# Second block's gate products: whole sums and weights' low parts by adding transfers; the last attention head at a denser pace

## The chip, the cores and the metric

One core of one Trainium2 chip runs the kernel. The metric is the device time of one execution in microseconds (us), the median of three runs. The engines are named as in the profile: PE is TensorE, DVE is VectorE, ACT is ScalarE, POOL is GpSimd, SP is SyncE, which only issues transfers here.

## The reference

Two transformer blocks follow one another, on 1024 positions of width 1024, all in float32. The change touches only the mixing part of the second:

```python
def second_block(x, ...):
    h = rms_norm_2(x, norm_mix_g)
    proj = h @ w_in
    (c_val, c_gate, g_q, g_k, g_v, g_og, g_f, d_q, d_k, d_v,
     m_conv, m_gla, m_diff) = jnp.split(proj, IN_OFFSETS, axis=-1)
    o_conv = conv_module(c_val, c_gate, ...)      # depthwise conv of 31, layer norm, silu, product
    o_gla = gla(g_q, g_k, g_v, g_og, g_f, ...)    # gated linear attention, 4 heads
    o_diff = diff_attention(d_q, d_k, d_v, ...)   # two softmaxes a head, 8 heads, rms norm of the output
    y = sigmoid(m_conv) * o_conv + sigmoid(m_gla) * o_gla + sigmoid(m_diff) * o_diff
    x = x + y @ w_out
    ...                                           # feed-forward, final norm
```

## The kernel before

Activations lie transposed in SBUF: a tile has 128 features on the partitions and 1024 positions along them, or a half of 512. A float32 operand is split into a high part, rounded to the matmul's type (`F32R`), and a low part, the rest. `mm3` makes a product of two split operands with three matmuls (high by high, high by low, low by high), so one 128x128 block of weights on 512 positions costs three matmuls. Two helpers make the parts. `split` (L379 to L382) casts on ScalarE and subtracts on VectorE or GpSimd. `split_dma` (L384 to L389) casts on ScalarE, lets ScalarE write the negated high part into the low part's tile, and lets GpSimd issue a transfer that adds the source to it.

The second block's mixing part has three stages. `diff` makes the differential attention and the projections that it and the convolution need. Its TensorE order is written by slots: a slot is half a product (12 matmuls), and `plan` hangs the steps of a head on slots: `scores`, three slots later `trans`, five later `pv` for every second block of queries, then `norm_sums` (it squares the head's output into `osq` and sums its columns on TensorE) and `norm_rows` (VectorE copies the factors to `bc`, TensorE turns them to rows `prow`). The other engines are ordered there by a planner, which works with its own costs. The last head has 24 slots; its norm rows hung on slots behind them.

`Gates` is next. It makes the remaining projections as 18 pairs of weight blocks, each pair by seven products of half size in place of eight. Products are taken of sums and differences of the blocks of the weights (`s1` to `s4`) and of the activations (`t1` to `t4`). `weights` makes one pair's: `part` splits two halves into a pair of tiles `hi`, `lo` (four buffers), `s2`, `s3`, `s4` are GpSimd's sums of raw weights, `w1` to `w4` call `part`. Raw weights have three buffers, filled in order by SP. `up` begins the stage: the activations lie split in `h`, so `full` adds the two parts of a block to a whole one (`g`, `a` in the profile), the differences are made on VectorE and split again. In between TensorE makes the forget gate's product (`forget`) and its four groups (`forget_up`, evacuated by ScalarE at L2481). `loop` then runs over the pairs, with the parts for the next pair made beside the products. In `Gates` the five engines' queues, SP's too, keep the order in which the program issues.

`Gla`, the gated linear attention, follows. The pools of `Gates` lie where those of `diff` were, so a tile of the one is free when the last reader of the other is done: `g1` and `g5` lie over the tile of `osq`.

The lines on which the change bears most, of `up` as it was:

```python
        W[0]["w1"]()
        f = self.forget_weights()
        sums(0)
        for t in ("s2", "s3", "s4"):
            W[0][t]()
        self.forget(*f)
        W[1]["w1"]()
        W[2]["w1"]()
        self.forget_up(0)
        sums(1)
        ...
        W[0]["w2"]()
        self.prod(0, 0)
```

Of the kernel before, what the change touches and what calls it, by code (L numbers as in the profile page):

```python
# [11 lines left out]
F32 = mybir.dt.float32  # L12
# [4 lines left out]
ALU = mybir.AluOpType  # L17
# [49 lines left out]
class Split:  # L67


    def __init__(self, pool, n, tag, halves=(0, 1)):  # L70
        self.pool, self.tag = pool, tag
        self.t = {h: [None] * n for h in halves}
        for h in halves:
            for i in range(n):
                self.make(h, i)
# [5 lines left out]
    def half(self, k, h):  # L81
        return self.t[h][k]
# [7 lines left out]
class Rope:  # L90
# [23 lines left out]
    def load(self, g, px, py):  # L114

        sx, sy, x, y = [self.tmp() for _ in range(4)]
        self.raw(px, self.net.v("qn_gx", 0), x, sx)
        for i, p in enumerate(py if isinstance(py, list) else ()):
            hs = slice(i * H, i * H + H)
            self.raw(p, self.net.v("qn_gy", 0), y[:, hs], sy[:, hs])  # L120
        if not isinstance(py, list):
            self.raw(py, self.net.v("qn_gy", 0), y, sy)
        self.xy[g] = x, sx, y, sy
# [161 lines left out]
class Net:  # L285
# [708 lines left out]
    def diff(self, hl, st, pre):  # L994
# [198 lines left out]
        def plan(h, base, pace):  # L1193

            s = [base + 4 + round(pace * qb) for qb in range(8)]
            for c in range(2):
                at(base + 3 + 2 * c, values, h, c)
            for qb in range(8):
                at(s[qb], scores, h, qb)
                at(s[qb] + 3, trans, h, qb)  # L1200
                if qb % 2:
                    at(s[qb] + 5, pv, h, qb // 2)
            at(s[7] + 7, norm_sums, h)
            at(s[7] + 12, norm_rows, h, 0)
            at(s[7] + 13, norm_rows, h, 1)

        def run(blocks):

# [24 lines left out]
        with tc.manual_schedule(engines={nc.tensor.engine}):  # L1233
            self.slot = -1
            run([("dq", 0), ("dk", 0)])
            self.slot = 0
            base = 0
            for h in range(8):
                blocks = head_blocks(h)
                plan(h, base, (1.5 if h == 0 else 1.7) if h in (0, 7) else 2)  # L1240
                run(blocks)
                base += 4 * len(blocks)
            for x in sorted(events):
                for f in events[x]:
                    f()
# [20 lines left out]
class Ending:  # L1266
# [17 lines left out]
    def plan(self, m, at, xT, tmp):  # L1284


        self.xT, self.tmp = xT, tmp
        at(0, lambda: self.net.w_fetch(3))
        for ct, x in enumerate((3 * m, 3 * m, 4 * m, 4 * m + 1)):
            at(x, lambda ct=ct: self.stat(0, ct))  # L1290
        at(5 * m - 1, self.warm)
        at(5 * m, lambda: self.stats(0, 4, 5))
        at(5 * m + 1, lambda: self.stats(0, 6, 7))
# [241 lines left out]
class Ffn:  # L1535
# [4 lines left out]
    UP = [("a11", "b11", "x", True), ("s2", "t2", "y", True), ("a12", "b21", "x", False), ("s3", "t3", "y", False),  # L1540
          ("s1", "t1", "z", True), ("a22", "t4", "y", False), ("s4", "b22", "z", False)]

    def __init__(self, net, g, nf, first_block, side):
        self.net, self.nc, self.g, self.nf, self.first_block = net, net.nc, g, nf, first_block
        self.side, self.other = (side, "left" if side == "right" else "right")
        self.xd = [net.dram.tile([P, S], F32, name=f"xd{nf}_{i}") for i in range(CT)]
        self.gd = [net.dram.tile([P, S], F32, name=f"gd{nf}_{i}") for i in range(nf)]
        self.n = 0
# [74 lines left out]
    def weights(self, j, A):  # L1623

        net, e = self.net, self.nc.gpsimd
        lo, hi = slice(0, H), slice(H, S)
        r, s = [], []

        def raw(i):
            while len(r) <= i:  # L1630
                net.w_fetch(1)
                r.append(net.wq_raw.pop(0)[1])
            return r[i]

        def part(names, srcs):
            h = net.whl.tile([P, S], F32R, tag="hi", name="whi")
            l = net.whl.tile([P, S], F32R, tag="lo", name="wlo")
            for o, src in srcs:
                net.split(h[:, o], l[:, o], src, e)
            for n, o in zip(names, (lo, hi)):  # L1640
                A[n] = h[:, o], l[:, o]

        def s2():
            s.extend(self.fw.tile([P, S], F32, tag=t, name=t) for t in ("sa", "sb"))
            self.tt(e, s[1][:, lo], raw(1)[:, lo], raw(1)[:, hi])
            self.tt(e, s[0][:, lo], s[1][:, lo], raw(0)[:, lo], ALU.subtract)
            net.w_fetch(1)

        def s3():
            self.tt(e, s[0][:, hi], r[0][:, lo], r[1][:, lo], ALU.subtract)  # L1650

        def s4():
            self.tt(e, s[1][:, hi], r[0][:, hi], s[0][:, lo], ALU.subtract)

        return {"w1": lambda: part(("a11", "a12"), [(lo, raw(0)[:, lo]), (hi, raw(0)[:, hi])]), "s2": s2, "s3": s3, "s4": s4,
                "w2": lambda: part(("s2", "s3"), [(slice(0, S), s[0])]),
                "w3": lambda: part(("s1",), [(lo, s[1][:, lo])]),
                "w4": lambda: (part(("s4", "a22"), [(lo, s[1][:, hi]), (hi, r[1][:, hi])]), net.w_fetch(2))}

# [744 lines left out]
class Gates(Ffn):  # L2404

    def __init__(self, net, hl, st):
        self.net, self.nc, self.hl, self.st = net, net.nc, hl, st
        self.nf = len(PAIRS)  # L2410
        self.more = []
        self.seen = set()
        self.n = 0
        self.other = "right"
        tiles = lambda n, m, w=S: [net.dram.tile([P, w], F32, name=f"{n}{i}") for i in range(m)]
        net.decd = tiles("decd", 4, 16)
        self.zd, net.xqd, net.xkd, net.kdd = [tiles(n, 4) for n in ("zd", "xqd", "xkd", "kdd")]
        net.gvd = [tiles(f"gvd{g}", 2) for g in range(4)]
        net.god = tiles("god", CT)
# [64 lines left out]
    def up(self):  # L2484
        net, nc, B, hl = self.net, self.nc, self.B, self.hl
        v, p = nc.vector, nc.gpsimd
        for k in range(4):
            for n, i, half in (("b11", k, 0), ("b21", k + 4, 0), ("b22", k + 4, 1), ("t1", k, 1)):
                B.setdefault(n, []).append(hl.half(i, half))
        self.pairs = {}  # L2490
        W = {}

        def new(j):
            A = {}
            W[j] = self.weights(j, A)
            self.pairs[j] = {"A": A}

        def full(e, o, x):
            self.tt(e, o, x[0].bitcast(F32), x[1].bitcast(F32))

        sub = lambda o, x, y: self.tt(v, o, x, y, ALU.subtract)
        half = lambda t: (t[:, 0:H], t[:, H:S])
        temps = half(self.big(1))
        t1 = half(self.big(5)) + half(self.T("a5"))

        def sums(k):
            x21, x22 = half(self.big(k % 2 * 4))
            x12 = temps[k % 2]
            full(p, x22, B["b22"][k])
            full(p, x21, B["b21"][k])  # L2510
            full(v if k < 2 else p, x12, B["t1"][k])
            full(v if k < 2 else p, t1[k], B["b11"][k])
            sub(t1[k], x12, t1[k])
            sub(x12, x22, x12)
            sub(x22, x22, t1[k])
            sub(x21, x21, x22)
            for n, t in (("t3", x12), ("t2", x22), ("t4", x21)):
                net.split(*B[n][k], t)

        for j in range(EARLY):  # L2520
            new(j)
        W[0]["w1"]()
        f = self.forget_weights()
        sums(0)
        for t in ("s2", "s3", "s4"):
            W[0][t]()
# [5 lines that stand above are left out]
        self.forget_up(1)  # L2532
        sums(2)
        self.forget_up(2)
        sums(3)
        W[0]["w2"]()
        self.prod(0, 0)

        for k in range(4):
            net.split(*B["t1"][k], t1[k])  # L2540
        self.prod(1, 0)
        self.prod(0, 2)
        W[0]["w3"]()
        self.forget_up(3)
        self.prod(1, 2)
        self.prod(2, 0)
        W[0]["w4"]()
        self.prod(2, 2)
        self.mask = self.tp.tile([P, S], BF16, tag="mask", name="mask")
        nc.gpsimd.memset(self.mask, 1.0)  # L2550
        nc.gpsimd.memset(self.mask.rearrange("p (n c) -> p n c", c=64)[:, :, 0:1], 0.0)
        self.prod(0, 1)
        self.evac(0, 0)
        self.evac(0, 2)
        self.prod(0, 4)
        self.evac(0, 1)
        self.prod(0, 3)
        self.evac(0, 4)
        return self.loop(W, new)
# [311 lines left out]
```

## Time and profile before

| | |
|---|---|
| median of 3 runs | 3532.34 us (3532.23 to 3535.09) |
| the profiled execution | 3533.49 us |
| its span in the profile | 3531.6 us |
| mean granted clock of TensorE | 0.967 |
| busy: TensorE, VectorE, ScalarE, GpSimd | 94%, 68%, 50%, 45% of the span |
| attention of the second block ends, last projection | about 2102 us |
| first product of the gate pairs | 2121 us |
| loop over pairs, to | about 2500 us |

The time of a run is some 2 us longer than the span, which runs from the first to the last instruction in the profile. A timeline row gives the start, the duration and what ended the engine's idle time before it. A granted clock of 1.00 is 2.4 GHz, 0.50 is 1.2 GHz.

### The profile page before, as it was taken

How to read it: one execution, taken by the hardware profiler on the slowest of the kernel's cores; microseconds unless marked ns; L12 is line 12 of the kernel's file. 1: busy time of each engine (PE TensorE's matmuls, PEld its weight loads, DVE VectorE, ACT ScalarE, POOL GpSimd, SP SyncE). 2: the span in 40 equal slices, each digit the busy share in tenths (PEclk: the TensorE clock that was granted, in tenths of full speed). 3: DMA queues.
4: the chain of work that ended last, by engine and by line, in shares of the span. 5: the costliest groups of instructions: out<-in, count | busy, mean ns of one | idle time of the engine just before them, and what ended most of it. 6: DMA issues, size and time to landing. Idle time of an engine off the chain costs nothing. (4 is left out here: it accounts for less than half of the span.)

```text
span 3531.6 us, 42519 instructions
## 1 busy us (share of the span) xinstructions
PE 3304.1 (94%) x15494; PEld 2707.7 (77%) x15494; DVE 2395.4 (68%) x3107; ACT 1751.7 (50%) x2851; POOL 1581.4 (45%) x1142
## 2 busy tenths in 40 slices
PE   7989997999999988999999999999998989999996
PEld 6768885888877776788888877777777768888775
DVE  7778848667667886777777755756477662222777
ACT  6548823444445644566666654545433233333565
POOL 2134318999942340000000018976443287776234
PEclk9989998999999998999999999999999999999998
DMA  4442231222258844444444423333555312223974
GB/s 132 96 122 61 68 109 45 90 84 78 90 173 220 198 114 104 99 105 107 108 111 109 102 73 107 132 132 124 193 185 191 129 62 78 84 84 107 259 176 110
DMA packets 137313, 419.41 MB, mean 119 GB/s; under 512 B 17072, under 2 KB 17456, under 8 KB 137104
## 3 DMA queue, kind: packets, MB, share of 16 engines
q1 hardware_dynamic: 92144, 297.58, 25.7%
q0 software_dynamic: 37904, 94.22, 13.4%
q10 hardware_dynamic: 7056, 24.91, 1.8%
q8 instruction: 122, 2.00, 0.2%
q14 instruction: 87, 0.71, 0.1%
HBM read 232.25 MB, written 84.97 MB: 90 GB/s over the span
## 5 line engine op out<-in xcount | busy, mean ns | idle before, releaser
L399 PE MATMUL pdn<-h,whi 128*128 128x512 f32 x1664 | 531.0, 400 | 1.0 <-ACT h L487 0.8
L382 POOL TENSOR_TENSOR wlo<-raw,whi 128x512 fp32r<-128x512 f32 (+1 forms) x211 | 331.0, 1581 | 252.8 <-ACT whi L381 251.1
L1554 DVE TENSOR_TENSOR f<-pf,f 128x512 f32<-128x512 f32 x224 | 154.0, 689 | 362.9 <-PE pf L399 362.3
L399 PEld LDWEIGHTS pdn<-h,whi 128*128 128x128 f32 x1664 | 308.5, 191 | 59.8 <-ACT h L487 1.2
L389 POOL DMA_DIRECT2D wlo<-raw x58 | 50.3, 874 | 635.7 <-ACT wlo L388 603.4
L399 PE MATMUL pdn<-h,wlo 128*128 128x512 f32 x832 | 329.5, 396 | 5.1 <-DMA wlo<-raw 5.1
L1039 DVE SCALAR_TENSOR_TENSOR cacc<-cu,vec,cacc 128x1024 f32<-128x1024 f32 x240 | 307.2, 1280 | 17.3 <-ACT cacc L1037 14.3
L399 PE MATMUL pd<-whi 128*128 128x512 f32 x644 | 258.3, 401 | 24.0 <-DVE f L1554 10.8
L399 PE MATMUL pd<-whi,wlo 128*128 128x512 f32 x644 | 259.2, 402 | 13.4 <-DMA wlo<-fs 7.6
L381 ACT CAST whi<-raw 128x512 fp32r<-128x512 f32 (+1 forms) x225 | 147.0, 681 | 229.5 <-PE pf L399 165.7
L399 PE MATMUL pd<-wlo,whi 128*128 128x512 f32 x644 | 256.8, 399 | 0.0
L381 ACT CAST whi<-sb 128x512 fp32r<-128x512 f32 x128 | 79.1, 620 | 338.3 <-PE pf L399 260.3
L382 POOL TENSOR_TENSOR wlo<-sb,whi 128x512 fp32r<-128x512 f32 x128 | 173.2, 1358 | 102.3 <-ACT whi L381 102.1
L382 POOL TENSOR_TENSOR wlo<-sa,whi 128x1024 fp32r<-128x1024 f32 x64 | 178.1, 2782 | 55.5 <-ACT whi L381 55.3
L399 PE MATMUL pf<-h,whi 128*128 128x512 f32 x576 | 182.7, 399 | 10.5 <-ACT a L2481 5.6
L399 PEld LDWEIGHTS pdn<-h,wlo 128*128 128x128 f32 x832 | 158.4, 190 | 40.6 <-DMA wlo<-raw 5.5
L399 PE MATMUL pp<-h,whi 128*128 128x512 f32 x448 | 150.8, 417 | 25.6 <-ACT h L535 10.8
L389 POOL DMA_DIRECT2D wlo<-fs x92 | 79.4, 865 | 194.4 <-ACT wlo L388 140.0
L399 PEld LDWEIGHTS pd<-whi 128*128 128x128 f32 x644 | 124.8, 194 | 53.2 <-ACT acc L1887 9.3
L388 ACT ACTIVATE wlo<-whi 128x512 fp32r<-128x512 f32 (+1 forms) x219 | 162.3, 742 | 5.4
L399 PEld LDWEIGHTS pd<-whi,wlo 128*128 128x128 f32 x644 | 124.4, 193 | 48.6 <-DMA wlo<-fs 12.5
L399 PEld LDWEIGHTS pd<-wlo,whi 128*128 128x128 f32 x644 | 124.6, 193 | 26.4
(566 smaller groups left out, 9636.6 us busy)
## 6 DMA issues: line engine op xcount, KB each, us to landing
raw<-in_w_in_dram SPq DMA_DIRECT2D x102, 512.0 KB, 3.6
wlo<-raw POOLq DMA_DIRECT2D x57, 512.0 KB, 4.6
raw<-in_w_up_dram SPq DMA_DIRECT2D x48, 512.0 KB, 3.5
gd<-f ACTq DMA_DIRECT2D x46, 512.0 KB, 2.6
fs<-gd SPq DMA_DIRECT2D x46, 512.0 KB, 7.0
wlo<-fs POOLq DMA_DIRECT2D x92, 256.0 KB, 4.7
raw<-in_w_ffn_in_dram SPq DMA_DIRECT2D x44, 512.0 KB, 3.5
wlo<-s POOLq DMA_DIRECT2D x69, 256.0 KB, 4.0
```

Of the source, the lines that this page charges most:

```text
L381: (copy or self.nc.scalar.copy)(hi, src)
L382: (eng or self.nc.vector).tensor_tensor(lo, src, hi.bitcast(F32), op=ALU.subtract)
L388: nc.scalar.activation(lo, hi.bitcast(F32), AF.Copy, scale=-1.0)
L389: nc.gpsimd.dma_start(lo.bitcast(F32), src, accum_op=ALU.add)
L399: nc.tensor.matmul(out, a, b, start=(first and i == 0), stop=(last and i == n - 1), skip_group_check=cont)
L1039: conv.append(lambda k=k: nc.vector.scalar_tensor_tensor(acc, u[:, k:k + S], cw(k), acc, op0=ALU.mult, op1=ALU.add))
L1554: e.tensor_tensor(o, x, y, op=op)
```

## The change

Four edits. The last attention head's scores go at a pace of 1.5 slots in place of 1.7, its norm rows on slots 9 and 10 behind the last scores in place of 12 and 13. In `Gates`, `part` makes the low parts of all weights with `split_dma` in place of GpSimd's subtraction. `full` makes a whole block by a copy that SP issues and an adding transfer that GpSimd issues, in place of a sum on GpSimd or VectorE; the loads of k = 0 and 1 are issued ahead of all sums, those of k = 2 and 3 behind the sums of k = 0 and 1. VectorE's differences are followed at once by ScalarE's casts, and the three low parts of a k come together at its end.

```diff
@@ -1201,8 +1201,8 @@
                 if qb % 2:
                     at(s[qb] + 5, pv, h, qb // 2)
             at(s[7] + 7, norm_sums, h)
-            at(s[7] + 12, norm_rows, h, 0)
-            at(s[7] + 13, norm_rows, h, 1)
+            at(s[7] + (12 if h < 7 else 9), norm_rows, h, 0)
+            at(s[7] + (13 if h < 7 else 10), norm_rows, h, 1)
 
         def run(blocks):
 
@@ -1237,7 +1237,7 @@
             base = 0
             for h in range(8):
                 blocks = head_blocks(h)
-                plan(h, base, (1.5 if h == 0 else 1.7) if h in (0, 7) else 2)
+                plan(h, base, 1.5 if h in (0, 7) else 2)
                 run(blocks)
                 base += 4 * len(blocks)
             for x in sorted(events):
@@ -1540,6 +1540,9 @@
     UP = [("a11", "b11", "x", True), ("s2", "t2", "y", True), ("a12", "b21", "x", False), ("s3", "t3", "y", False),
           ("s1", "t1", "z", True), ("a22", "t4", "y", False), ("s4", "b22", "z", False)]
 
+
+    quiet = False
+
     def __init__(self, net, g, nf, first_block, side):
         self.net, self.nc, self.g, self.nf, self.first_block = net, net.nc, g, nf, first_block
         self.side, self.other = (side, "left" if side == "right" else "right")
@@ -1636,7 +1639,10 @@
             h = net.whl.tile([P, S], F32R, tag="hi", name="whi")
             l = net.whl.tile([P, S], F32R, tag="lo", name="wlo")
             for o, src in srcs:
-                net.split(h[:, o], l[:, o], src, e)
+                if self.quiet:
+                    net.split_dma(h[:, o], l[:, o], src)
+                else:
+                    net.split(h[:, o], l[:, o], src, e)
             for n, o in zip(names, (lo, hi)):
                 A[n] = h[:, o], l[:, o]
 
@@ -2405,6 +2411,8 @@
 
 
 
+    quiet = True
+
     def __init__(self, net, hl, st):
         self.net, self.nc, self.hl, self.st = net, net.nc, hl, st
         self.nf = len(PAIRS)
@@ -2495,32 +2503,44 @@
             W[j] = self.weights(j, A)
             self.pairs[j] = {"A": A}
 
-        def full(e, o, x):
-            self.tt(e, o, x[0].bitcast(F32), x[1].bitcast(F32))
+        def full(o, x):
+            nc.sync.dma_start(o, x[0].bitcast(F32))
+            p.dma_start(o, x[1].bitcast(F32), accum_op=ALU.add)
 
         sub = lambda o, x, y: self.tt(v, o, x, y, ALU.subtract)
         half = lambda t: (t[:, 0:H], t[:, H:S])
         temps = half(self.big(1))
         t1 = half(self.big(5)) + half(self.T("a5"))
-
-        def sums(k):
+        whole = {}
+
+        def load(k):
+
             x21, x22 = half(self.big(k % 2 * 4))
             x12 = temps[k % 2]
-            full(p, x22, B["b22"][k])
-            full(p, x21, B["b21"][k])
-            full(v if k < 2 else p, x12, B["t1"][k])
-            full(v if k < 2 else p, t1[k], B["b11"][k])
+            for o, n in ((x12, "t1"), (t1[k], "b11"), (x22, "b22"), (x21, "b21")):
+                full(o, B[n][k])
+            whole[k] = x21, x22, x12
+
+        def sums(k):
+            x21, x22, x12 = whole.pop(k)
             sub(t1[k], x12, t1[k])
-            sub(x12, x22, x12)
-            sub(x22, x22, t1[k])
-            sub(x21, x21, x22)
-            for n, t in (("t3", x12), ("t2", x22), ("t4", x21)):
-                net.split(*B[n][k], t)
+            lows = []
+            for n, t, x in (("t3", x12, x22), ("t2", x22, x22), ("t4", x21, x21)):
+                sub(t, x, {"t3": x12, "t2": t1[k], "t4": x22}[n])
+                h, l = B[n][k]
+                nc.scalar.copy(h, t)
+                lows.append((l, t, h.bitcast(F32)))
+            for x in lows:
+                sub(*x)
+            if k < 2:
+                load(k + 2)
 
         for j in range(EARLY):
             new(j)
         W[0]["w1"]()
         f = self.forget_weights()
+        load(0)
+        load(1)
         sums(0)
         for t in ("s2", "s3", "s4"):
             W[0][t]()
```

## Rows read from the trace of the kernel before

**Rows 1.** The page: busy us (share of the span), instructions of each engine.
```profile
PE 3304.1 (94%) x15494; PEld 2707.7 (77%) x15494; DVE 2395.4 (68%) x3107; ACT 1751.7 (50%) x2851; POOL 1581.4 (45%) x1142
```

**Rows 2.** Windows by stretch: start:end, length, each engine's busy us, PEclk, DMA share, GB/s.
```profile
2101.00:2115.00 14.00, 9.79 (x40) 4.80 (x39) 9.10 (x18) 4.01 (x6) 0.59 (x1) 0.88 0.19 76
...
2115.00:2130.00 15.00, 14.79 (x56) 10.69 (x55) 10.39 (x7) 5.05 (x9) 12.40 (x9) 0.89 0.09 35
...
2130.00:2145.00 15.00, 9.39 (x33) 6.76 (x32) 14.79 (x15) 5.44 (x10) 9.91 (x6) 0.77 0.17 70
...
2205.00:2285.00 80.00, 74.33 (x316) 58.10 (x315) 62.97 (x45) 45.14 (x59) 72.81 (x36) 1.00 0.37 131
```

**Rows 3.** Timeline of PE: start, us, instruction, [idle before <-releaser].
```profile
2097.23 1.84 PE L437 MATMUL pst<-onef,osq 128*128 128x1 f32 x16
...
2104.89 0.63 PE L453 MATMUL prow<-ident,bc 128*128 128x128 f32 x4 [2.94 <-DVE bc L444]
...
2106.78 0.64 PE L453 MATMUL prow<-ident,bc 128*128 128x128 f32 x4 [1.27 <-DVE bc L444]
...
2141.32 1.22 PE L399 MATMUL pf<-h,whi 128*128 128x512 f32 x2 [5.61 <-ACT a L2481]
...
2150.52 0.50 PE L399 MATMUL pf<-t2h,whi 128*128 128x512 f32 x1 [1.86 <-ACT a L2481]
...
2165.98 0.39 PE L399 MATMUL pf<-t2h,whi 128*128 128x512 f32 x1
...
2168.73 0.63 PE L399 MATMUL pf<-h,whi 128*128 128x512 f32 x2
...
2349.42 0.65 PE L399 MATMUL pf<-t3h,whi 128*128 128x512 f32 x1 [2.97 <-DVE g L1554]
```

**Rows 4.** Windows of 1 us for PE: busy, PEclk, DMA share, GB/s.
```profile
2121.00:2122.00 1.00, 1.00 (x4) 0.50 0.95 385
...
2122.00:2123.00 1.00, 1.00 (x4) 0.50 0.35 139
```

**Rows 5.** Timeline of DVE.
```profile
2099.19 0.68 DVE L1554 TENSOR_TENSOR g<-h 128x512 f32<-128x512 f32 x1
...
2117.63 3.50 DVE L1554 TENSOR_TENSOR g<-h 128x512 f32<-128x512 f32 x2
...
2146.80 0.69 DVE L382 TENSOR_TENSOR t4l<-g,t4h 128x512 fp32r<-128x512 f32 x1
```

**Rows 6.** Timeline of POOL.
```profile
2083.67 1.29 POOL L1554 TENSOR_TENSOR sb<-raw 128x512 f32<-128x512 f32 x1 [7.09 <-PE ptr L1144]
...
2117.60 6.35 POOL L382 TENSOR_TENSOR wlo<-raw,whi 128x512 fp32r<-128x512 f32 x4 [6.97 <-ACT whi L381]
```

**Rows 7.** Timeline of SP, which issues transfers.
```profile
2087.89 6.76 SPq L354 DMA_DIRECT2D raw<-in_w_in_dram  x2
```

**Rows 8.** Transfers issued: engine, count, KB each, median us to landing.
```profile
wlo<-raw POOLq DMA_DIRECT2D x57, 512.0 KB, 4.6
...
raw<-in_w_in_dram SPq DMA_DIRECT2D x102, 512.0 KB, 3.6
...
wlo<-s POOLq DMA_DIRECT2D x69, 256.0 KB, 4.0
...
swp<-qb SPq DMA_DIRECT2D x8, 256.0 KB, 2.9
```

**Rows 9.** Queues and issues in 1080:1250: packets, MB, share of 16 engines.
```profile
q0 software_dynamic: 8631, 15.71, 53.9%
...
wlo<-fs POOLq DMA_DIRECT2D x34, 256.0 KB, 5.0
```

**Rows 10.** Lines of split_dma: duration ns min/median/max, first and last start, forms.
```profile
L389 POOL DMA_DIRECT2D wlo<-fs x92: 859/859/1120, 1017.8 to 3483.8; - x92
...
L388 ACT ACTIVATE wlo<-whi x219: 311/632/1107, 56.6 to 3494.3; 128x512 fp32r<-128x512 f32 x81, 128x1024 fp32r<-128x1024 f32 x29
```

**Rows 11.** What PE waited for in 1350:1450, head 0: us, times, longest.
```profile
PE psc L1118 <- ACT e L1125: 2.7, 2, 2.2
```

## The prediction

> **What bounds the kernel now.** The views, in this order. The page's busy times [rows 1]: TensorE works 94% of the span, so only stretches where it waits or runs slowly can give time back. The windows by stretch [rows 2] find them near the change: from 2101 to 2145, 44 us, it is busy 34, part of that at a low granted clock. The timeline of TensorE [rows 3] names the waits. Two are at the end of attention, 2.94 and 1.27 us for VectorE's broadcast columns `bc`; then 5.61 and 1.86 for ScalarE's forget columns, which free the PSUM banks; at 2349 it is 2.97 for a VectorE sum. After a wait the clock drops to its lower level, 1.2 GHz [rows 4], about 3.4 us each time, during which half the work is done: 1.7 us lost. The timeline of VectorE [rows 5] says why ScalarE is late: a sum of two SBUF operands takes 1.75 us while GpSimd works and 0.69 otherwise, and ScalarE's casts stand in order behind those sums. Last the queues: GpSimd's and SP's timelines [rows 6, 7], the landings of transfers [rows 8, 9] and the lines of a split [rows 10].
>
> **The mark.** Product 1 of pair 1, the first `t2` product at 2165.98 [rows 3], begins right when GpSimd's low part of its weights is done; with the next pairs TensorE then goes on unbroken. I work out when it begins after the change, then what the rest of the loop gains.
>
> **Attention's end.** The column sums of `osq` end at 2099.07 and are issued two slots earlier; a slot is 12 matmuls, 2.75 us (from 2165.98 to 2168.73 [rows 3]), so they end 5.5 us earlier. The last row products now lie among projections. Their first `bc` came 5.8 us after the sums, with VectorE's sums of k = 0 in between, which are gone from there; two slots cover what is left, one slot the second `bc`: both waits vanish, 4.2 us. Against it stand three scores in three slots. Head 0 has this pace: its scores waited 2.7 us for ScalarE [rows 11], the last pair 0.5 of it (the rest belongs to its early blocks). I take 1, bounds 0 and 2.7. The sums then end at E = 2099.1 - 5.5 + 1 = 2094.6. E counts because `g1` and `g5`, first destination of the loads, can't be written before: the old first write there came at 2099.19 [rows 5], right behind these sums. Should the planner set VectorE's new sums ahead of the second `bc`, TensorE's forget products come some 6 us later; they are ready well before what bounds the route below, so that costs nothing unless the route is shorter.
>
> **Loads for k = 0 and 1.** Removed are GpSimd's and VectorE's 16 whole sums. Added are 16 copies on SP's queue and 16 adds on GpSimd's. No row has such a pair; nearest are a 256 KB copy between tiles, landed 2.9 us after issue, an add, 4.0 [rows 8], and its issue, 0.86 [rows 10]. The transfer engines need per add, 128 packets, 53.9% of 170 us x 128 / 8631 = 1.36 us [rows 9], per copy half of a 512 KB write's 1.3 [rows 4], 0.65. Eight of both need 16.1 us from E + 2; k = 0 is whole at E + 10 if its own go first, near E + 16 if all share. I take 13; below 9 it can't be, since four issues and one landing follow a first copy (2.9 + 3 x 0.86 + 4.0 = 9.5).
>
> **A new wait, and what stands behind it.** The sums of k = 0 (2.4 us with their low parts) free the tiles into which k = 2 is copied. GpSimd's queue holds k = 2's adds ahead of `s2`, `s3`, `s4` of pair 0, and SP's holds k = 2's copies ahead of both weight loads behind them. So SP: four issues and a landing, 5 us; GpSimd's last add is issued at T = E + 13 + 2.4 + 5 + 0.9 = E + 21.3 = 2115.9. Before, these sums began at 2083.67 and the weight loads at 2087.89 [rows 6, 7]. The Trainium skill says in DMA: Bandwidth & Descriptors, Anatomy of one DMA — SWDGE (gpsimd) path, that DMA engines don't wait on semaphores, the issuing sequencer does. By that, an add that waits for its copy holds all of GpSimd's queue; no row here shows one that waits so. Were the queue free meanwhile, the four sums would keep their old place, the second load too, and the mark would be bounded by TensorE.
>
> **From T to the mark.** GpSimd's four sums, 4 x 1.29: T + 5.2. They free the buffer for pair 2's weights: loaded 3.6 later [rows 8], T + 9. ScalarE stands in order: pair 2's first parts now cost cast, negated copy, twice, at 0.6 each [rows 10]: T + 11.5; forget columns (two passes) 1.3, three casts of k = 1's sums 1.6: T + 14.4. k = 3 is loaded behind them: four copies and adds, T + 24; its casts T + 25.5. Then pair 0's `w2` 2.1, `t1` 2.1, `w3` 1.2, forget columns 1.3, `w4` 2.4: T + 34.6. Its last add lands 4.0 later, T + 38.6, and only then is pair 1's second weight loaded, 3.6; three GpSimd sums 3.9; cast and negation 2.1; 512 KB added 4.6 [rows 8]: T + 52.8 = 2168.7. Against 2165.98: **2.7 late**. TensorE alone would be there some 6 us sooner, so it waits and its clock drops, **1.7**. Thus +4.4, though VectorE's sums of k = 3 end some 5 us before their old 2147.5 [rows 5]: without GpSimd's whole sums beside them, they are done, and the longer route of the weights (an add's 4.0 instead of a subtraction's 1.6 [rows 6], and a negation) gives it back. Bounds: E + 10 and no stall in the scores, 2.7 - 3 - 1 = -1.3 (TensorE alone would give -4); E + 16, adds 1 us slower at three places of the route, 2.7 us of stall in the scores and the clock, 2.7 + 3 + 3 + 1.7 + 1.7 = +12.
>
> DMA: Bandwidth & Descriptors (same section of the Trainium skill) fits a transfer as 2.0 us plus bytes over 436 GB/s, an estimated 2.6 us for 256 KB. The rows have 4.0 to 5.0 for adds of this size and decide; by the Trainium skill's fit the mark would come some 6 us sooner, bounded by TensorE.
>
> **The loop, 18 pairs.** GpSimd loses six subtractions a pair (seven times 512 columns at 1.3 to 1.6) and gets six issues of 0.86. ScalarE gets six negations, 5 x 0.6 + 1.06 = 4.1 us a pair; at 2205 to 2285 it has 45 of 80 us over four pairs [rows 2], so 15.4 of 20: it still fits, and the work that hides it is TensorE's. Weights are made four products (11 us) ahead of use and need 2.4 + 0.9 + 4.6 = 8: hidden by 3 us; a landing of 8 us would uncover it. The transfers' share: 7 x 1.36 = 9.5 us a pair onto 0.37 x 20 = 7.4 [rows 2], nearly full in places, harmless if loads keep a pair's lead. Gains: VectorE's normalization sums fall as in [rows 5], by about 1 us each, but wait longer for ScalarE's squares, pushed by two negations (1.2): the 2.97 becomes about 1.5, short enough to keep the clock (waits of that kind stand in 2205 to 2285, 5.7 us in all, and the clock stayed at 1.00 there), 3.1 us for each of two halves, -6. In the forget-gate pairs 5.7 us of waits stand in 80 [rows 2]; VectorE saves, ScalarE's logarithm comes 1.2 later: -1. Evacuating copies of ScalarE that slip behind negations: +2, bounds 0 and 8 (18 x 0.45). The loop: **-5**, bounds -12 and +5.
>
> **Sum.** 4.4 - 5 = -0.6 on the profiled execution's 3533.5 (span 3531.6 and 1.9 around it); it lies 1.2 above the median, so 3531.8 on the median 3532.3. 0.2%, 7 us, is what the measurement can tell from no change.
>
> **Rivals.**
> *Loads early, loop freed* (faster). k = 0 is whole by E + 10 or the adds land near 3 us, the mark comes 2 to 4 us early, and both normalization halves lose wait and slow clock alike (2 x 5): 3532 - 13 = 3519. For it: VectorE's rows alone and beside GpSimd differ by 1 us a sum. Against: ScalarE's order. Chance 0.29. It is also where the fit of the Trainium skill's DMA: Bandwidth & Descriptors would lead; the landings of 4 us bear that out little.
> *The route of the weights* (slower). One mechanism: pair 0's buffers wait for landings. If adds land at 5 to 6 us while the copies share the engines, the five landings behind E give 1 to 2 us each, the mark comes 10 late and pair 2 follows 2 late: 3532 + 12 - 3 = 3541. It decides from landings of 5 us. For it: 5.0 stands in a stage where the engines are this busy [rows 9]. Chance 0.18.
> *ScalarE sets the pace of the loop* (slower). Negations ahead of its evacuating copies, 8 to 10 us over 18 pairs and no gain at the normalization: 3544. Against: 15.4 of 20. Chance 0.08.
> *Moved but hidden*: the forecast. Chance 0.45; its own range is 3526 to 3538.
>
> So 3532, range 3519 to 3543: about 0.1 lies under, as much over. Faster by 0.2%: 0.29; within: 0.45; slower: 0.26.
>
> **What would show it.** After: no wait for `bc` before the row products; VectorE's sums of k near 0.69; `s2` of pair 0 after 2110 and two weight loads behind it; a wait of about 6 us before the first product on pair 1's `t2`, named by the weights' add; at the two normalizations waits under 2 us and a clock of 1.00. Wrong it is if that product starts before 2163 or after 2175, or if ScalarE's copies release TensorE over and over in the loop.

## The result, and the profile after

The changed kernel takes 3573.66 us (median; 3563.88 to 3574.34, 4 runs), the kernel before beside it 3532.82 (4 runs): ratio 1.0104, 95% interval 1.0091 to 1.0117. It is 41 us slower and outside the predicted range of 3519 to 3543. The profiled execution took 3574.01 us, its span 3572.2, 40.6 above the span before.

The page, the row that answers to [rows 1]; GpSimd and VectorE lost work, ScalarE got 71 us more:

```profile
PE 3316.6 (93%) x15494; PEld 2712.5 (76%) x15494; DVE 2341.1 (66%) x3103; ACT 1822.7 (51%) x2957; POOL 1478.9 (41%) x1146
```

TensorE's timeline at the end of attention and at the start of the stage, which answers to [rows 3]:

```profile
2073.46 0.55 PE L1144 MATMUL ptr<-ident,e 128*128 128x128 f32 x3 [1.67 <-DVE tl L382]
2079.38 1.09 PE L1144 MATMUL ptr<-ident,e 128*128 128x128 f32 x8 [0.52 <-DVE tl L382]
2094.11 1.84 PE L437 MATMUL pst<-onef,osq 128*128 128x1 f32 x16
...
2134.05 0.79 PE L399 MATMUL pf<-h,wlo 128*128 128x512 f32 x1 [6.40 <-DMA wlo<-raw]
...
2158.01 0.79 PE L399 MATMUL pf<-t2h,whi 128*128 128x512 f32 x1 [5.94 <-ACT a L2489]
...
2174.76 0.39 PE L399 MATMUL pf<-t2h,whi 128*128 128x512 f32 x1
2180.70 0.79 PE L399 MATMUL pf<-t2h,wlo 128*128 128x512 f32 x1 [5.32 <-DMA wlo<-sa]
```

The waits for `bc` are gone. In their place stand waits for low parts that a transfer has still to deliver. The windows (columns as in [rows 2]) show what is new there: the transfer engines' share, 0.09 to 0.19 before and 0.37 in the loop.

```profile
2101.00:2115.00 14.00, 12.12 (x56) 6.90 (x54) 7.91 (x12) 3.21 (x6) 6.26 (x8) 1.00 1.09 233
2115.00:2130.00 15.00, 12.29 (x31) 8.89 (x31) 3.59 (x6) 2.39 (x4) 9.93 (x10) 0.65 0.89 221
2130.00:2145.00 15.00, 10.95 (x34) 8.23 (x35) 6.47 (x10) 8.02 (x15) 5.36 (x7) 0.67 0.91 250
...
2222.00:2305.00 83.00, 76.36 (x327) 60.25 (x326) 50.69 (x44) 64.25 (x85) 42.03 (x40) 1.00 0.87 216
```

The queues at the start: GpSimd's, SP's and ScalarE's timelines, a fence each. They answer to [rows 6, 7].

```profile
2098.89 0.86 POOL L2508 DMA_DIRECT2D g<-h  x1 [20.12 <-DMA g<-h]
...
2120.00 0.85 POOL L2508 DMA_DIRECT2D g<-h  x1 [6.99 <-DMA g<-h]
...
2121.23 2.26 POOL L2508 DMA_DIRECT2D g<-h  x2
2122.41 2.40 POOL L1557 TENSOR_TENSOR sb<-raw 128x512 f32<-128x512 f32 x1
```

```profile
2095.99 5.20 SPq L2507 DMA_DIRECT2D g<-h  x8
...
2113.55 0.46 SPq L2507 DMA_DIRECT2D g<-h  x1
...
2118.06 10.95 SPq L354 DMA_DIRECT2D raw<-in_w_in_dram  x2
```

```profile
2122.60 0.62 ACT L387 CAST whi<-raw 128x512 fp32r<-128x512 f32 x1 [7.81 <-DMA raw<-in_w_in_dram]
...
2132.77 0.62 ACT L387 CAST whi<-raw 128x512 fp32r<-128x512 f32 x1 [7.72 <-DMA raw<-in_w_in_dram]
```

Everything that ScalarE has behind these two casts (forget columns, casts of k = 1) is late with them. In the loop, from 2180 to 2545, the low parts land later than the 4.0 to 4.6 us that [rows 8] gave. Transfers by tile: count, KB, median us to landing; then what SP's weight loads, GpSimd's sums and VectorE's convolution waited for in 2180 to 2500 (us in all, times, longest):

```profile
q0 software_dynamic: 13984, 29.63, 45.7%
...
wlo<-raw POOLq DMA_DIRECT2D x47, 256.0 KB, 6.0
wlo<-sb POOLq DMA_DIRECT2D x33, 256.0 KB, 6.5
wlo<-sa POOLq DMA_DIRECT2D x16, 512.0 KB, 6.1
```

```profile
SPq L354 <- DMA wlo<-raw: 137.0, 24, 9.7
```

```profile
POOL sb L1557 <- DMA wlo<-sb: 37.9, 10, 6.7
```

```profile
DVE a L1557 <- DMA a<-cvd: 19.9, 9, 4.8
```

The reader is to see three holds by one landing: TensorE's, the raw buffer's (SP can't load the next weights) and that of `sb` (GpSimd can't write the next sum, and its queue stands). Not all of SP's 137.0 us is new: before, the same loads waited 104.8 us for GpSimd's sums and subtractions (69.3 and 35.5), now 157.2 with the 20.2 that are left of those. The last fence shows that other transfers are late as well: VectorE waits 19.9 us for the convolution's reloads `cvd`, before not at all. TensorE's waits in the loop, of the kinds that repeat:

```profile
2213.25 0.50 PE L399 MATMUL pf<-h,wlo 128*128 128x512 f32 x1 [1.39 <-DMA wlo<-raw]
...
2229.93 0.50 PE L399 MATMUL pf<-t4h,whi 128*128 128x512 f32 x1 [1.03 <-DVE g L1557]
...
2381.31 0.51 PE L399 MATMUL pf<-t3h,whi 128*128 128x512 f32 x1 [3.01 <-DVE g L1557]
```

The last answers to 2349.42 in [rows 3]: the wait of 2.97 at the normalization, which was to become 1.5, is unchanged.

Two stretches split the time. The **start** goes from the squares of attention's head 6, which no edit touches (2006.49 before, 2004.99 after), to the first product on pair 1's `t2`. The **loop** goes from there to pair 17's first `t2` product (2494.90 before, 2534.15 after). Before: 159.5 and 328.9 us. After: 169.8 and 359.4; the wait of 5.32 at 2180.70, behind that product's first two matmuls, counts to the loop. So 10 us were lost at the start, 30 in the loop. What lies outside the two stretches is 3043 us in both traces.

### The profile page after: what moved, and what is told of

Same layout as the page of the kernel before. It is cut to its first block, busy times and chain, and to the rows that moved or that the text cites. A ratio compares the mean times of both kernels' runs of the same rounds, so it can differ in the third digit from the quotient of the medians.

```text
span 3572.2 us, 42759 instructions
## 1 busy us (share of the span) xinstructions
PE 3316.6 (93%) x15494; PEld 2712.5 (76%) x15494; DVE 2341.1 (66%) x3103; ACT 1822.7 (51%) x2957; POOL 1478.9 (41%) x1146
## 5 line engine op out<-in xcount | busy, mean ns | idle before, releaser
L389 POOL DMA_DIRECT2D wlo<-raw x112 | 98.0, 907 | 674.6 <-ACT wlo L388 631.8
L382 POOL TENSOR_TENSOR wlo<-raw,whi 128x512 fp32r<-128x512 f32 (+1 forms) x157 | 251.3, 1613 | 212.4 <-ACT whi L381 211.0
L1039 DVE SCALAR_TENSOR_TENSOR cacc<-cu,vec,cacc 128x1024 f32<-128x1024 f32 x240 | 307.1, 1280 | 17.3 <-ACT cacc L1037 14.3
L388 ACT ACTIVATE wlo<-whi 128x512 fp32r<-128x512 f32 (+1 forms) x327 | 238.3, 729 | 8.8
L381 ACT CAST whi<-raw 128x512 fp32r<-128x512 f32 (+1 forms) x171 | 115.5, 702 | 201.9 <-PE pf L399 141.5
L381 ACT CAST whi<-sb 128x512 fp32r<-128x512 f32 x92 | 56.9, 620 | 251.3 <-PE pf L399 188.8
L387 ACT CAST whi<-raw 128x1024 fp32r<-128x1024 f32 (+1 forms) x112 | 92.9, 831 | 134.1 <-PE pdn L399 84.4
L382 POOL TENSOR_TENSOR wlo<-sb,whi 128x512 fp32r<-128x512 f32 x92 | 121.9, 1328 | 71.1 <-ACT whi L381 71.1
L1557 DVE TENSOR_TENSOR g<-pf,g 128x512 f32<-128x512 f32 x93 | 63.8, 687 | 129.7 <-PE pf L399 110.1
```

Source lines behind the costliest of these rows:

```text
L381: (copy or self.nc.scalar.copy)(hi, src)
L382: (eng or self.nc.vector).tensor_tensor(lo, src, hi.bitcast(F32), op=ALU.subtract)
L387: nc.scalar.copy(hi, src)
L388: nc.scalar.activation(lo, hi.bitcast(F32), AF.Copy, scale=-1.0)
L389: nc.gpsimd.dma_start(lo.bitcast(F32), src, accum_op=ALU.add)
L1039: conv.append(lambda k=k: nc.vector.scalar_tensor_tensor(acc, u[:, k:k + S], cw(k), acc, op0=ALU.mult, op1=ALU.add))
```

## The experiments

All were timed in five rounds, in four groups with the kernel before beside each: 3532.97 us for e1 to e4, 3533.86 for e5 to e8, 3533.05 for e9 to e12, 3535.58 for e13 to e15. "Start" and "loop" are the stretches above, from each kernel's own trace. A trace is one execution, up to 9 us off its kernel's median. Most of that lies outside the two stretches, where the seventeen traces have 3036 to 3049 us in no order by edit. The loops of the seven kernels that leave the loop's low parts to GpSimd as before, and change nothing else in it, lie between 328.8 and 333.5 us: two loops can differ by 4.7 us without an edit to the loop.

| kernel | median us | ratio to before, 95% interval | start | loop |
|---|---|---|---|---|
| before | | | 159.5 | 328.9 |
| the change | 3573.66 | 1.0104 (1.0091 to 1.0117) | 169.8 | 359.4 |
| e1 attention alone | 3529.08 | 0.9984 (0.9976 to 0.9993) | 156.7 | 330.4 |
| e2 low parts alone | 3566.11 | 1.0092 (1.0077 to 1.0107) | 163.0 | 357.7 |
| e3 loads and sums alone | 3538.80 | 1.0019 (1.0010 to 1.0028) | 166.1 | 328.8 |
| e4 ScalarE's passes alone | 3554.39 | 1.0057 (1.0045 to 1.0069) | 164.9 | 340.1 |
| e5 e3, `s2` to `s4` first | 3533.92 | 0.9997 (0.9988 to 1.0005) | 158.8 | 333.5 |
| e6 e2 without the passes | 3547.68 | 1.0038 (1.0026 to 1.0050) | 163.3 | 338.3 |
| e7 e6 with plain copies | 3516.93 | 0.9949 (0.9937 to 0.9960) | 152.0 | 317.9 |
| e8 e1 and e5 | 3534.95 | 1.0000 (0.9991 to 1.0009) | 157.3 | 330.3 |
| e9 e2, raw halves only | 3541.93 | 1.0022 (1.0014 to 1.0031) | 160.5 | 331.7 |
| e10 e2, passes on VectorE | 3578.29 | 1.0129 (1.0115 to 1.0143) | 169.2 | 367.0 |
| e11 e1, all low parts by VectorE | 3566.74 | 1.0098 (1.0084 to 1.0112) | 150.9 | 373.3 |
| e12 e1, raw low parts by VectorE | 3551.83 | 1.0053 (1.0040 to 1.0066) | 149.0 | 355.5 |
| e13 change, transfers in the loop only | 3568.62 | 1.0094 (1.0079 to 1.0109) | 164.0 | 357.1 |
| e14 change, transfers at the start only | 3548.83 | 1.0037 (1.0025 to 1.0050) | 169.7 | 330.4 |
| e15 e12, at the start only | 3524.36 | 0.9971 (0.9959 to 0.9982) | 149.6 | 330.9 |

**e1, e2, e3: each edit by itself.** e1 is the diff's first two hunks; e2 is `quiet = True` with the old sums and pace; e3 is the new `load` and `sums` with `quiet = False`.

> Only the last attention head's pace and its norm rows are changed; whole sums and weights' low parts stay as before. The two waits for bc, 4.2 us, should be gone and one slow stretch of TensorE's clock with them. Theory that the loss lies with the transfers alone: 3529 to 3533, at best 4 us under before, since the first products of the gate pairs still wait for ScalarE behind VectorE's sums. Theory that the denser head itself costs (it shows 2.2 us of waits for VectorE's low parts): 3533 to 3536.

> Only the low parts of the weights of the 18 gate pairs go by negated copy and adding transfer; sums and attention as before. If the transfers' share (0.87 in the loop after, 0.37 before) carries the loss: 25 us or more over before, 3555 to 3562, with adds landing after 6 us and TensorE waiting for wlo. If ScalarE's 96 added passes carry it, the same time here, but then the run with the passes and without the transfers shows it too. If most of the loss comes from the whole sums at the start: under 3540 here.

> Only the whole sums go by copy and adding transfer, with the new order of sums; low parts of weights stay on GpSimd, attention as before. The first t2 product of pair 1 came 14.7 us late after the full change. If the queues behind the loads cause that (GpSimd's sums of weights and two weight loads stand behind the transfers for k = 2): 6 to 12 us over before, 3539 to 3545, and the loop as before. If it is the low parts' longer route: within 3 us of before.

Attention gains 4 us, the loads lose 6, the low parts lose 33: nearly all of it. (ScalarE has 108 more instructions in e2, six for each of 18 pairs, not 96.) In e1 one of the waits for `bc` is left, at 0.23 us. In e3 ScalarE waits for raw weights at the start, which SP could fetch only behind the copies for k = 2 (ScalarE's timeline, then SP's):

```profile
2125.82 1.14 ACT L381 CAST whi<-raw 128x512 fp32r<-128x512 f32 x2 [7.88 <-DMA raw<-in_w_in_dram]
2135.37 1.14 ACT L381 CAST whi<-raw 128x512 fp32r<-128x512 f32 x2 [8.41 <-DMA raw<-in_w_in_dram]
```

```profile
2118.93 2.74 SPq L2507 DMA_DIRECT2D g<-h  x2
2121.76 10.34 SPq L354 DMA_DIRECT2D raw<-in_w_in_dram  x2
```

**e4: the passes without the transfers.** ScalarE writes the negated copy, then GpSimd subtracts over it as before. The two lines that matter:

```diff
+        nc.scalar.activation(lo, hi.bitcast(F32), AF.Copy, scale=-1.0)
         eng.tensor_tensor(lo, src, hi.bitcast(F32), op=ALU.subtract)
```

> ScalarE writes the negated high part into the low part's tile, as with the adding transfers, but GpSimd then subtracts over it as before, so the transfers stay as before and ScalarE has all of its added passes; sums and attention as before. Theory that ScalarE's order makes the loop slow: 3545 to 3560, most of what the run with the transfers shows. Theory that the transfers do: 3531 to 3538.

21 us with no transfer added: the theory that the transfers alone did it falls. The trace has 5.4 of them at the start and 11.2 in the loop. One pair of the forget gate in ScalarE's timeline of e4:

```profile
2231.11 0.60 ACT L386 CAST whi<-raw 128x512 fp32r<-128x512 f32 x1
2231.74 0.63 ACT L387 ACTIVATE wlo<-whi 128x512 fp32r<-128x512 f32 x1
2232.28 0.61 ACT L386 CAST whi<-raw 128x512 fp32r<-128x512 f32 x1
2232.92 0.63 ACT L387 ACTIVATE wlo<-whi 128x512 fp32r<-128x512 f32 x1
2233.57 1.28 ACT L2700 ACT_TABLE_LOAD   x1
2234.86 1.06 ACT L2700 ACTIVATE a<-a 128x1024 f32<-128x1024 f32 x1
```

and what follows on VectorE and TensorE:

```profile
2235.96 1.23 DVE L2701 SCALAR_TENSOR_TENSOR a<-a,a 128x1024 f32<-128x1024 f32 x1 [3.61 <-ACT a L2700]
2237.10 0.68 DVE L1562 TENSOR_TENSOR g<-pf,g 128x512 f32<-128x512 f32 x1
```

```profile
2237.84 0.50 PE L405 MATMUL pf<-t4h,whi 128*128 128x512 f32 x1 [1.31 <-DVE g L1562]
```

ScalarE does not pause from 2230.14 to 2242.07. The activation at 2234.86 (L2700) stands behind the negations; VectorE waits for it, VectorE's evacuation of a PSUM bank (L1562) stands behind that wait, and TensorE waits for the bank. ScalarE's 59 busy us of 83 in 2222 to 2305 (43 before) are not the bound as an average; in this pair the order is. That it is so in all pairs is not shown. It fits that TensorE's waits in 2180 to 2500 rise from 14.3 to 21.6 us, every one of them for VectorE or ScalarE and none for a low part.

**e5, e8: the start's queues.**

```diff
+        for t in ("s2", "s3", "s4"):
+            W[0][t]()
         load(0)
         load(1)
         sums(0)
-        for t in ("s2", "s3", "s4"):
-            W[0][t]()
```

> The loads and sums edit alone, as in e3_loads, but GpSimd's sums s2 to s4 of the first pair (and the fetch of raw weights behind them) are issued ahead of the loads for k = 0 and 1. Queue theory: in e3 SP's two raw weight loads stood behind the copies for k = 2 (issued at 2121.8 in place of 2087.9) and ScalarE waited 7.9 and 8.4 us for them with the forget columns and the casts of k = 1 behind it; so the first product on pair 1's t2 comes back from 75 us behind the column sums of attention to 62 to 69 us, and the time is 3526 to 3532 us. Rival, the loads themselves (16 copies and adds on the transfer engines, landing late) set the start: it stays within 3 us of e3, 3536 to 3541 us.

> The attention edit and e5_order together, low parts by GpSimd as before: the gains add if they are independent. Queue theory: 3522 to 3529 us. If the loads themselves set the start: 3532 to 3538 us.

With GpSimd's sums ahead, and with them the first of the two weight loads (the second still stands behind the copies for k = 2, at 2123.39), the start returns from 166.1 to 158.8: the queue was the loss. Both times came out higher than the queue theory gave, though: freed of it, the loads gain nothing over the old sums, and the attention edit's gain can't be seen on top.

**e6, e7: the transfers without the passes.** In e6 the transfers add onto four kept tiles that nothing else writes; in e7 they copy. The low parts are then running sums of the sources, or the sources. The lines below are a cut, against e2; e6's first four parts are made as in e2, and e7's tiles take turns as in e2.

```diff
-                    net.split_dma(h[:, o], l[:, o], src)
+                    net.nc.scalar.copy(h[:, o], src)
+                    net.nc.gpsimd.dma_start(l[:, o].bitcast(F32), src, accum_op=ALU.add)  # e7: no accum_op
```

> The low parts by adding transfers alone, as in e2_lows, but from the fifth part on the transfer adds onto one of four low tiles that are kept and written by nothing else, so that ScalarE makes no negated copy (low parts are then running sums of the sources, not the rests). Transfers, their sizes, GpSimd's issues and all waits for landings stay as in e2. If ScalarE's second pass carries two thirds of the loss, as e4_negs suggests: 3540 to 3548 us. If the waits for landings carry it on their own (source buffers and first uses held 6 us): 3555 to 3566 us.

> As e6_nopass, but the transfer is a plain copy of the source into the low tile (low parts are then the sources): the same issues and waits, about half the work for the transfer engines. If the engines' share makes the landings late and these the loss: landings fall from about 6 to 3 to 4 us and the time lies 8 us or more under e6_nopass, near 3536 to 3542. If the share is harmless, as predicted: within 3 us of e6_nopass.

The passes are worth 3566 - 3548 = 18 us, in line with e4's 21. The adds in place of copies cost 3548 - 3517 = 31; e7 lies far under the 3536 to 3542 that were expected. Without either, taking the subtractions from GpSimd gains 17. In the loop alone the passes cost 11.2 us without the adds (e4) and 19.4 on top of them (e2 against e6). The transfers in 2180 to 2500, of e6:

```profile
q0 software_dynamic: 12856, 27.13, 47.3%
...
wlo<-raw POOLq DMA_DIRECT2D x46, 256.0 KB, 5.9
wlo<-sa POOLq DMA_DIRECT2D x15, 512.0 KB, 7.7
wlo<-sb POOLq DMA_DIRECT2D x30, 256.0 KB, 7.3
```

and of e7:

```profile
q0 software_dynamic: 7812, 26.30, 21.3%
...
wlo<-raw POOLq DMA_DIRECT2D x43, 256.0 KB, 2.6
wlo<-sb POOLq DMA_DIRECT2D x29, 256.0 KB, 3.1
wlo<-sa POOLq DMA_DIRECT2D x14, 512.0 KB, 2.9
```

Nearly the same bytes take 47.3% of the engines' time as adds and 21.3% as copies, and copies land in less than half the time. VectorE also waits 17.3 us for the convolution's reloads `cvd` in e6, 1.5 in e7. They land 6.9 us after their issue, in e7 6.4, so SP seems to issue them late, behind weight loads that wait. How the 20.4 us of the loop divide between such waits and those for the weights is not shown.

**e9: three of a pair's seven halves.** Transfers for raw sources, GpSimd's subtraction for sums of weights.

> The low parts by adding transfers for the halves of raw weights alone (three of a pair's seven), those of the sums s1 to s4 by GpSimd's subtraction as before; nothing else changed. If the loss is in proportion to passes and transfers: three sevenths of e2's 33 us, 3547 us. If the transfers cost only where the engines' share nears 0.9 and landings pass 5 us (share here about 0.37 plus 3 adds of 1.5 in 20 us, 0.6, as in e7_plain), what is left is three sevenths of the passes' 18 us, less what GpSimd's relief gives back (17 us in e7 for all seven): 3531 to 3538 us.

Between the two theories. Adds at 0.63 of the engines land in 4.0 us, and TensorE waits for them 0.8 us in all: little of the transfers' part is left, as the share theory says. Where the 9 us that stay come from is open: the trace has 1.0 at the start and 2.8 in the loop, no more than two loops differ without an edit. Three sevenths of the passes' 18, without the relief that I had set against it, would be 8.

**e10, e11, e12: other engines for the work.** e10: `nc.vector.tensor_scalar(..., -1.0)` makes the negated copy. e11, e12: `net.split` on VectorE.

> As e2_lows, but VectorE writes the negated copies in place of ScalarE. If the passes cost because of ScalarE's order (casts, evacuating copies and logarithms behind them), the 18 us go and 3545 to 3551 us stay, as e6_nopass. If any second pass between cast and transfer costs it, by the chain cast, negation, issue, landing, or VectorE's own order is as tight: 3558 to 3570 us.

> The attention edit, and the low parts of all weights of this stage by VectorE's subtraction in place of GpSimd's; no transfers, no second pass. e7_plain showed what GpSimd's relief is worth, some 17 us, when nothing takes its place. VectorE has 56 of 83 us there; 28 subtractions of 0.69 make 75 of 83 if they stand alone, over 100 if each takes 1.7 beside GpSimd's sums. If they mostly stand alone: 3518 to 3528 us, under both kernels. If VectorE's order becomes the bound: 3540 us or more.

> As e11_vsub, but only the raw halves (three of seven) by VectorE. A third of GpSimd's relief, VectorE at 56 plus 8 to 20 of 83 us: 3522 to 3530 us if the relief counts, 3532 to 3540 us if VectorE's waits for ScalarE's casts hold up its evacuations.

All three lose in the loop, e10 and e12 more than either of their theories gave. The traces name one wait in all three. What VectorE waited for in 2180 to 2500, of e10, e11 and e12; then GpSimd, of the kernel before:

```profile
DVE wlo L1643 <- ACT whi L1642: 75.4, 35, 4.6
```

```profile
DVE wlo L382 <- ACT whi L381: 82.2, 34, 4.9
```

```profile
DVE wlo L382 <- ACT whi L381: 51.6, 18, 4.8
```

```profile
POOL wlo L382 <- ACT whi L381: 65.9, 31, 5.9
```

ScalarE's cast itself waits for TensorE to free the `hi` tile (109.2 us in e11, 103.4 before). Whoever makes the low part waits along, in order; GpSimd could stand there, VectorE has evacuations behind it: TensorE's waits for VectorE in that stretch are 39.9 us in e11 and were 13.2. Busy time (VectorE 59 of 83 us in e11) says nothing of it. But e12 starts the loop 10 us early, 8 more than attention's edit does by itself.

**e13, e14, e15: start and loop apart.** The edits alone sum to 35 of the 41 us, so the parts were also put in one stage at a time, by setting `quiet` where `loop` begins. e15 is e12 with VectorE's subtractions ahead of the loop only.

> The whole change, but the low parts by adding transfers in the loop over pairs alone; in the stage before it (all first parts, pair 0) GpSimd subtracts as before. The three edits by themselves make 35 us (minus 4, 6 and 33) of the change's 41. If the missing 6 arise at the start, where loads and low parts share queues and transfer engines, the first product on pair 1's t2 comes 163 us behind head 6's squares (before's 159.5 plus 6.6 of the loads less 2.8 of attention) and the loop keeps its 359 us in place of 329: 3562 to 3567 us. If they arise in the loop, the time falls only by the low parts' own 3 to 9 us at the start and the loop is under 355 us.

> The counterpart: the whole change, but in the loop GpSimd subtracts as before. If the loss of the start and of the loop add up: start near 170 to 175 us, loop 329 to 334 us, together with e13 some 41 us over before; so 3540 to 3549 us. If the start's lateness is hidden by the loop's: under 3538 us.

> The attention edit alone, and ahead of the loop the raw weights' low parts by VectorE in place of GpSimd; in the loop GpSimd subtracts. e12_vsubraw started the loop 149 us behind head 6's squares in place of 159.5, and lost it in the loop by VectorE's waits for ScalarE's casts. If start and loop are independent: start 149 to 152, loop 329 to 331, 3523 to 3527 us, under both kernels. If GpSimd's order hands the gain back in the first pairs: 3528 to 3533 us.

Start and loop add up: e14's 169.7 and e13's 357.1 are, to 2.3 us, the change's 169.8 and 359.4. The start holds 3 us more than the three edits give by themselves (159.5 - 2.8 + 6.6 + 3.5 = 166.8); the other 3 of the missing 6 aren't located, and the intervals of the four ratios, of 3 to 5 us each way, could hold all six. e15 beats both kernels, by 0.29% the one before and, by the two ratios, 1.3% the changed one: its row is what remains of this change once the losing parts are left out, with the start's low parts on an engine that is free there. Over e1 its start is 7 us shorter in the trace; in the times the two intervals overlap.

## Why the prediction was wrong

The step that failed is "The loop": -5 with bounds -12 to +5, measured +30.5, or +25 without the wait of 5.3 that the prediction counts at the mark. Two of its terms, ScalarE and transfers, went by busy shares where the order of the work decides. The terms, by e2, e6 and e7 in the loop alone:
- *Gains*: predicted -7, measured 317.9 - 328.9 = -11. Right in kind, too small: the two pairs with a normalization give 7.0 where 6 was forecast, their wait of 2.97 becomes 1.54 and 1.39 in e7, as worked out, and the other pairs give 4.1 in place of 1. In the change itself the two waits are 3.01 and 3.00.
- *ScalarE*: "15.4 of 20: it still fits", +2, bounds 0 and 8. Measured 357.7 - 338.3 = +19.4 on top of the adds, 16 without the wait at the mark, and 11.2 by themselves (e4). The average itself was right, 64.25 of 83 us or 15.5 of 20, but a wrong test: activations for which VectorE waits stand in order behind the negations, and VectorE's evacuations behind those.
- *Transfers*: "nearly full in places, harmless if loads keep a pair's lead", 0. Measured 338.3 - 317.9 = +20.4, 18 without the wait at the mark. The share itself was right, 0.85 worked out and 0.87 measured. "Hidden by 3 us" counted one landing ahead of use; the same landing also holds the raw buffer and `sb`, and VectorE waits for the convolution's reloads. That the next pair begins later by these holds is argued from the waits: no run loosens one of them by itself.

The rival *ScalarE sets the pace of the loop*, at 0.08, named one half of this at 8 to 10 us: close to the 11.2 of the passes alone, half of what they cost beside the adds. Its "no gain at the normalization" came true. But it put the loss on ScalarE's evacuating copies; the releases of TensorE by them are 2.8 us in 2180 to 2500, so the sign "over and over in the loop" did not come.

*The mark*, +4.4 predicted: its first low-part matmul went from 2166.44 to 2180.70, +14.3. The prediction's own sign, a start of that product between 2163 and 2175, was just met at 2174.76, but the product stopped after two matmuls. The route was right, the sizes at its head and tail were not. E came at 2095.95 (2094.6 predicted). k = 2's copies were issued at 2113.55, 3.5 us late, 1.4 of it by E and the rest behind the head's last products on VectorE; the first add followed them 6.5 us later in place of 2.9, with the engines' share at 0.89 to 1.09. So the last add was issued at T = 2123.5, not 2115.9. From there GpSimd's sums (T + 5.1), pair 2's weights (T + 9.3) and k = 1's casts (T + 14.4) came as worked out (5.2, 9, 14.4); from k = 3's loads on, 4.4 more were lost, most of it to landings. The clock's price of 1.7 came as worked out: 0.50 granted from 2178 to 2184, with 3.3 us of TensorE's work in it, and 0.88 in the microsecond after. But the 3.4 us that the prediction gives a slow stretch are not all there is: 0.65 and 0.67 in 2115 to 2145, where 0.89 and 0.77 stood in [rows 2], are two stretches of 10 us at 1.2 GHz, the first, from 2116, with TensorE busy throughout. They lie off the route, since TensorE waits again at 2158.

That GpSimd's queue stands while an add waits for its copy, which no row had shown, is shown now: 6.99 us at 2120.00, with `s2` behind it. So the Trainium skill's rule that the issuing sequencer does the waiting (DMA: Bandwidth & Descriptors, Anatomy of one DMA — SWDGE (gpsimd) path) agrees with this trace. The same section's fit, an estimated 2.6 us for 256 KB, agrees with e7's copies of that size (2.6 and 3.1) and not with the adds (4.0 to 7.3).

*Attention's end*, -4.2 with 1 us of stall: both waits vanished as said, but the sums came only 1.6 us earlier against head 6 (89.1 in place of 90.7 us), not 4.5, so 3.9 were lost where 1 was taken, with a bound of 2.7. TensorE's idle time between the two marks rises from 1.3 to 4.4 us, 2.2 of it for VectorE's `tl` and 2.2 for ScalarE's `e`; the other 0.8 isn't located. That e1 still gains 3.9 us is not this sum come true: its trace has 2.8 of them at the start.

*The route of the weights* (0.18, 3541) was part of the mechanism of the start: late landings behind E, 3.6 us at k = 2's copies and most of the last 4.4. The other part is the forecast's own, GpSimd's and SP's queues behind the loads; e3 and e5 bear that out, 7 us of the start from the order alone.

## What to carry to other kernels

Busy shares don't price work that is added to an in-order engine: list what stands behind it in one period, and who waits for that. A transfer that replaces an operation of an engine holds its source and its target until it lands, so count the buffers' next writers and not only the reader, at the landing time of the stage as it will be loaded then. Split an edit by part and by stage before judging it: here attention's gain of 0.16% stood beside the low parts' loss of 0.9%, and raw low parts off GpSimd shortened the start (e15) and lost in the loop (e12).

## What the runs showed of the hardware

An adding transfer between SBUF tiles takes the 16 engines 0.473 x 320 us x 0.262 / 27.13 MB = 1.46 us per 256 KB (e6), a plain copy 0.213 x 320 x 0.262 / 26.30 = 0.68 (e7). In 2180 to 2500 the median landing of 256 KB adds goes from 4.0 us at a share of 0.63 (e9) to 5.9 and 7.3 at 0.88 (e6), while copies land in 2.6 and 3.1 at 0.62 (e7). VectorE's sums of two SBUF tensors took 0.69 us each at the start of the changed kernel, now without GpSimd's sums beside them, as [rows 5] let expect:

```profile
2106.30 0.69 DVE L1557 TENSOR_TENSOR g<-g,g 128x512 f32<-128x512 f32 x1 [3.19 <-issue]
```
